# First layer norm of a decoder trunk: row statistics of two of three token chunks moved from VectorE's statistics instruction to ScalarE's accumulating passes

## The chip, the core and the metric

The kernel runs on one core of a Trainium2 chip. TensorE multiplies matrices out of SBUF into PSUM, VectorE and ScalarE do the elementwise work, GpSimd does a little of it, and the queue of SyncE starts nearly all transfers. The metric is the device time of one execution in microseconds. The time before is 1571.87 us, the median of three runs (1571.16 to 1574.35).

## The reference, cut to what matters

One decoder layer is computed for 1024 prompt tokens and 32 sample tokens, together 1056 tokens of 1024 features. A head mixer (mLSTM and sparse attention) gives `mixed`; the change touches only the layer norm behind it.

```
x = layer_norm(ALPHA * x + g1 * mixed, ln_g[0], ln_b[0])
u2 = x * (1 + sc2) + sh2
ff = jnp.square(jax.nn.relu(u2 @ w_up)) @ w_down
x = layer_norm(ALPHA * x + g2 * ff, ln_g[1], ln_b[1])

def layer_norm(x, g, b):
    mu = x.mean(-1, keepdims=True)
    var = jnp.square(x - mu).mean(-1, keepdims=True)
    return (x - mu) * lax.rsqrt(var + LN_EPS) * g + b
```

## The kernel before

Activations lie transposed, features on the partitions. The 1056 tokens are cut into three chunks, c = 0, 1 and 2, of 384, 384 and 288 tokens. For each chunk the following is done.

- `wout_steps(c)` multiplies by w_out: eight output tiles, m = 0 to 7. Each of the eight weight tiles comes by a transfer into the single buffer `wst`, is cast by ScalarE into `wo..h` (L50), and VectorE writes the rest of the split into `wo..l` (L51). TensorE makes `po` (L354), VectorE adds the residual into `y` (L1135).
- `ln1(c)` first takes the chunk in tiles of up to 128 tokens, three to a chunk. For each tile TensorE transposes the eight `y` into two PSUM halves `pn` of 128x512 (L1245). Of these halves there are four buffers, so two tiles can be under way. Then `norm_rows` takes the statistics: VectorE's statistics instruction on each half (L1246), their aggregation (L1251), the addition of the epsilon (L113), GpSimd's power of -1/2 (L114), and VectorE's -mean*r (L1253). Last, ScalarE writes the normalised tile `xna` from the two halves (L1267). There are three `xna` buffers, as many as a chunk has tiles, so the tiles of a chunk reuse the buffers of the chunk before.
- The second half of `ln1(c)` is a loop over the eight feature tiles f: TensorE transposes back from the three `xna` into `pb` (L1301, two buffers), ScalarE applies gain and bias into `x1` (L1303, two buffers, named `x` in the rows), a transfer stores `x1` to `d_x1` (L1304), VectorE makes `uraw` (L1307), and ScalarE and VectorE split it into the operands `B11`, `B21`, `B22`. Behind chunks 1 and 2 sums of blocks (`t_sum`, L1364) follow, which the up-projection's seven products need.

A second form, `norm_rows_act`, is in use in the second layer norm at the end of the kernel, where the tiles are named `xnf` and `lstf`. It takes the sum of a half as a by-product of a copying ScalarE pass (L1276), makes minus the mean on VectorE (L1280), takes the sum of squares as a by-product of a ScalarE Square pass with minus the mean as its bias (L1282), makes variance, root and -mean*r (L1284, L113, L114, L1286), and then writes the normalised tile as the first form does (L1288). Both of the extra passes write their elementwise result into the tile `xn` as well, where the final pass overwrites it:

```python
ACT.activation(xn[0:rows, 512 * hf:512 * hf + 512], pts[hf][0:rows], AF.Identity,
               accum_out=st[0:rows, hf:hf + 1])
...
ACT.activation(xn[0:rows, 512 * hf:512 * hf + 512], pts[hf][0:rows], AF.Square, bias=nm,
               accum_out=s[:, 3 + hf:4 + hf])
```

The order of the calls in the program is `ln1(0)`, the rest of `wout_steps(1)`, `ln1(1)`, `wout_steps(2)`, `ln1(2)`, and then `up_early` for two of the up-projection's column blocks (`pu0e`, `pu1e`), whose products with `B11` and `B21` can begin before chunk 2 is done. When the program is built, the framework's planner puts the instructions of each engine in an order from a timeline that it simulates, with the program's order as priority; on the chip each engine then runs its list in order and waits where an operand isn't there.

Of the kernel before, what the change touches and what calls it, by code (L numbers as in the profile page):

```python
# [47 lines left out]
def split(nc, hi, lo, src):  # L48

    nc.scalar.copy(hi, src)  # L50
    nc.vector.tensor_tensor(out=lo, in0=src, in1=hi.bitcast(F32), op=ALU.subtract)  # L51
# [7 lines left out]
def _body(tc, nc, top, io, dbg):  # L59
    PE, ACT, DVE, POOL, SP = nc.tensor, nc.scalar, nc.vector, nc.gpsimd, nc.sync  # L60

    def pool(name, stack, bufs=1, space=None, side=None):
        kw = {}
        if space is not None:
            kw["space"] = space
        if side is not None:
            kw["side"] = side
        if space is not DRAM:
            kw["reuse_waits"] = "tile"
        return stack.enter_context(tc.tile_pool(name=name, bufs=bufs, **kw))  # L70

    def mk(p, shape, dt, tag, bufs=None, name=None):
        kw = {} if bufs is None else {"bufs": bufs}
        return p.tile(list(shape), dt, tag=tag, name=name or tag, **kw)
# [16 lines left out]
    def v4(x, t=4):  # L91
        return x.rearrange("p (b t) -> p b t", t=t)

    def bc(x, n):

        return x.unsqueeze(2).broadcast_to([x.shape[0], x.shape[1], n])
# [131 lines left out]
    for i in range(16):  # L228
# [5 lines left out]
        if i % 2:  # L234
            o = kvx[:, :, 8 * i - 8:8 * i + 8].rearrange("p x (a n) -> p a x n", a=2)
# [590 lines left out]
    for h in range(2):  # L826
# [23 lines left out]
        for j in range(2):  # L850
            o, p = 512 * j, 288 * j
# [278 lines left out]
    ys = {}  # L1130
# [42 lines left out]
    while not (qs.end and qp.end and dn_end):  # L1173
# [4 lines left out]
        if best <= t and (behind or dn_at > t):  # L1178
            if rp <= t:
                qp.need = None  # L1180
                c = qp.pull()
            else:
                qs.need = None
                c = qs.pull()
# [54 lines left out]
    p4 = pool("p4", s4_, side="right")  # L1239
    ps4 = pool("ps4", s4_, space=PSUM)  # L1240

    def norm_half(pts, st, cols, hf, rows):

        for x in range(4):
            PE.transpose(pts[hf][0:rows, 128 * x:128 * x + 128], cols[4 * hf + x], ident)  # L1245
        DVE.bn_stats(st[0:rows, 6 * hf:6 * hf + 6], pts[hf][0:rows])  # L1246

    def norm_stats(st, rows):

        mv, rs = st[0:rows, 12:14], st[0:rows, 14:16]  # L1250
        DVE.bn_aggr(mv, st[0:rows, 0:12])  # L1251
        rstd_of(rs[:, 0:1], mv[:, 1:2], EPA)
        DVE.tensor_scalar(rs[:, 1:2], mv[:, 0:1], rs[:, 0:1], -1.0, op0=ALU.mult, op1=ALU.mult)  # L1253
        return mv[:, 0:1], rs[:, 0:1], rs[:, 1:2]

    def norm_tiles(pp, name):
        return (mk(pp, [128, 1024], F32, "xn", bufs=3, name=f"xn{name}"),
                mk(pp, [128, 16], F32, "lst", bufs=3, name=f"lst{name}"))

    def norm_rows(pp, pts, name, cols, rows):  # L1260

        xn, st = norm_tiles(pp, name)
        for hf in range(2):
            norm_half(pts, st, cols, hf, rows)
        _, r, nmr = norm_stats(st, rows)
        for hf in range(2):
            ACT.activation(xn[0:rows, 512 * hf:512 * hf + 512], pts[hf][0:rows], AF.Identity, scale=r, bias=nmr)  # L1267
        return xn
# [22 lines left out]
    def ln1(c):  # L1291
        t0, n = CH[c]
        tts = [(o, min(128, n - o)) for o in range(0, n, 128)]
        xns = []
        for o, rows in tts:
            pts = [mk(ps4, [128, 512], F32, "t", bufs=4, name=f"pn{c}{o}{hf}") for hf in range(2)]
            xns.append(norm_rows(p4, pts, f"a{c}{o}", [ys[c, m][:, o:o + rows] for m in range(8)], rows))
        for f in range(8):
            pt = mk(ps4, [128, 512], F32, "t2", bufs=2, name=f"pb{c}{f}")
            for (o, rows), xn in zip(tts, xns):  # L1300
                PE.transpose(pt[:, o:o + rows], xn[0:rows, 128 * f:128 * f + 128], ident[0:rows, 0:rows])  # L1301
            x1 = mk(p4, [128, 384], F32, "x1", bufs=2, name=f"x1{c}{f}")
            ACT.activation(x1[:, 0:n], pt[:, 0:n], AF.Identity, scale=lnT[:, 0, f:f + 1], bias=lnT[:, 1, f:f + 1])  # L1303
            SP.dma_start(d_x1[:, f, t0:t0 + n], x1[:, 0:n])  # L1304
            u = uraw[:, f, t0:t0 + n]
            np_ = min(n, 1024 - t0)
            DVE.tensor_scalar(u[:, 0:np_], x1[:, 0:np_], sc2p[:, f, 0:1], ada[:, 3, f, 0:1], op0=ALU.mult, op1=ALU.add)  # L1307
            if np_ < n:
                DVE.tensor_tensor(out=v4(u[:, np_:n]), in0=v4(x1[:, np_:n]), in1=bc(sc2p[:, f, 1:9], 4), op=ALU.mult)
                DVE.tensor_tensor(out=v4(u[:, np_:n]), in0=v4(u[:, np_:n]), in1=bc(ada[:, 3, f, 1:9], 4), op=ALU.add)  # L1310
            for a, b, name in ((t0, min(t0 + n, TH), "B21" if f >= 4 else "B11"), (max(t0, TH), t0 + n, "B22")):
                if a < b and (a < TH or f >= 4 and c < 2):
                    hi, lo = (x[:, f % 4, a % TH:a % TH + b - a] for x in ops[name])
                    split(nc, hi, lo, uraw[:, f, a:b])
            if f >= 4 and c:
                a, b = ((0, 240), (240, TH))[c - 1]
                t_sum("T3", f - 4, a, b, POOL if c == 1 else DVE)
                t_sum("T2", f - 4, a, b, POOL if c == 1 else DVE)
                if c == 2 and f < 4 + KT:
                    split(nc, ops["T2"][0][:, f - 4], ops["T2"][1][:, f - 4], ublock("T2", f - 4, 0, TH))  # L1320
# [37 lines left out]
    def ublock(name, k, a, b):  # L1358
        f, t = blk[name]
        return uraw[:, f + k, t + a:t + b]  # L1360

    def t_sum(name, k, a, b, eng):
        x, y, op = sum_of[name]
        eng.tensor_tensor(out=ublock(name, k, a, b), in0=ublock(x, k, a, b), in1=ublock(y, k, a, b), op=op)  # L1364

    TENG = POOL
    ln1(0)
    for _ in fill or wout_steps(1):
        pass
    ln1(1)  # L1370
    for _ in wout_steps(2, pq):
        pass
    operand(pq, "T2")
    ln1(2)
    spre = ExitStack()
    ppre = pool("pre", spre)
# [291 lines left out]
    def banks(name):  # L1668
        nt[0] += 1
        return [wtile(f"pnf{name}{hf}") if nt[0] % 2 else mk(psd, [128, 512], F32, "t", bufs=2, name=f"pnf{name}{hf}")  # L1670
                for hf in range(2)]
# [35 lines left out]
    pts = [banks(t) for t in last]  # L1707
    xns = [norm_tiles(pf, f"f{t}") for t in last]
# [149 lines left out]
```

## Time and profile before

| | |
|---|---|
| time, median of 3 runs | 1571.87 us |
| the profiled execution's time | 1571.22 us |
| its span | 1569.5 us |
| busy share: TensorE, VectorE, ScalarE, GpSimd | 95%, 67%, 42%, 19% |
| first layer norm, first transposition to last `x1` | 785.95 to 857 us |

The page gives shares over the whole span. The layer norm is one stretch of 71 us in it, which the windows and timelines below show by itself. The profiled execution took 1.7 us more than its span, and lies 0.65 us below the median.

### The profile page before, as it was taken

What the parts mean: (1) busy time and instruction counts of PE and PEld (TensorE: products, weight loads), DVE (VectorE), ACT (ScalarE), POOL (GpSimd) and SP (SyncE); (2) the same over time, 40 slices, a digit from 0 to 9 for tenths busy, and PEclk for the clock granted to TensorE, in tenths of its full rate; (3) what the DMA queues carried; (4) which work ended last, traced back from release to release, by engine and by line L of the source; (5) the groups of instructions that cost most, each with busy time, mean ns of one, the idle gap of its engine ahead of it and who ended that gap; (6) DMA issues with size and microseconds to landing.
All of it is one profiled execution on the core that took longest, in us unless ns stands there. A gap on an engine that the chain in (4) does not pass through costs nothing.

```text
span 1569.5 us, 30107 instructions
## 1 busy us (share of the span) xinstructions
PE 1492.4 (95%) x11647; PEld 1433.4 (91%) x11647; DVE 1054.1 (67%) x2340; ACT 657.6 (42%) x1332; POOL 300.6 (19%) x387
## 2 busy tenths in 40 slices
PE   6899999999999999899998799999999999998985
PEld 5788988999999998798897799999999999998985
DVE  2421132386676677977688887767668788979867
ACT  2422132375665566645466322222226433333363
POOL 0000000143224243443103300000001120304044
PEclk9989999999999999999999899999999999999997
DMA  8757477521020323323564566323323341422352
GB/s 294 276 188 266 115 195 243 149 73 48 26 78 19 98 67 120 89 61 102 170 215 137 188 217 221 110 99 108 103 83 129 136 150 56 131 88 54 111 107 85
DMA packets 112987, 204.11 MB, mean 130 GB/s; under 512 B 18530, under 2 KB 63499, under 8 KB 111915
## 3 DMA queue, kind: packets, MB, share of 16 engines
q1 hardware_dynamic: 109242, 196.67, 38.6%
q0 software_dynamic: 2304, 4.20, 1.8%
q8 instruction: 92, 1.51, 0.4%
q10 hardware_dynamic: 1296, 1.31, 0.2%
q14 instruction: 53, 0.43, 0.1%
HBM read 162.95 MB, written 46.07 MB: 133 GB/s over the span
## 4 chain that ended last, share of the span: by engine, by line
PE 75%; DVE 12%; DMA 6%; issue 3%; ACT 2%; POOL 1%; SPq 1%; ACTq 0%; DVEq 0%; POOLq 0%
PE p L1329 20%; PE pj L354 15%; PE pd L1564 11%; PE po L354 6%; PE o L1060 4%; PE pt L1019 4%; PE S L979 4%; DMA wada<-in_w_ada 3%; PE pA L298 2%; DVE oplT L51 2%; DVE ophT L51 2%; DVE A L1575 2%; PE ada L149 1%; DVE acc L1569 1%; PE hidS L277 1%
## 5 line engine op out<-in xcount | busy, mean ns | idle before, releaser
L1564 PE MATMUL pd<-oplT,ophT 128*128 128x264 f32 x2352 | 291.9, 287 | 8.5 <-ACT acc L1583 4.4
L1564 PEld LDWEIGHTS pd<-oplT,ophT 128*128 128x128 f32 x2352 | 290.9, 190 | 9.4 <-DVE ophT L51 4.8
L1002 POOL TENSOR_SCALAR P<-P,l,sg 128x64 f32<-128x64 f32 (+8 forms) x192 | 129.1, 686 | 173.7 <-DVE l L999 154.8
L51 DVE TENSOR_TENSOR PTl<-pt,PTh 128x512 fp32r<-128x512 f32 (+1 forms) x160 | 101.9, 643 | 31.2 <-ACT PTh L50 30.6
L996 ACT ACTIVATE P<-P,mn 128x640 f32<-128x640 f32 (+7 forms) x128 | 94.3, 737 | 67.7 <-DVE mn L823 64.3
L354 PE MATMUL pj<-uh,wt_l 128*128 128x384 f32 (+1 forms) x576 | 120.3, 333 | 0.0
L50 ACT CAST PTh<-pt 128x512 fp32r<-128x512 f32 (+1 forms) x160 | 86.7, 550 | 79.7 <-PE pt L1019 78.9
L354 PE MATMUL pj<-uh,wt_h 128*128 128x384 f32 (+1 forms) x576 | 115.9, 331 | 0.7 <-ACT rw L468 0.7
L354 PE MATMUL pj<-ul,wt_h 128*128 128x384 f32 (+1 forms) x576 | 116.5, 329 | 0.0
L1575 POOL TENSOR_TENSOR A<-A,A 128x1024 f32<-128x1024 f32 x7 | 24.1, 3455 | 476.7 <-DVE ophT L51 475.5
L50 ACT CAST ophT<-A 128x1024 fp32r<-128x1024 f32 x49 | 51.3, 1049 | 133.7 <-PE pd L1564 85.5
L354 PEld LDWEIGHTS pj<-uh,wt_l 128*128 128x128 f32 x576 | 95.7, 190 | 2.8 <-issue 2.4
L1019 PE MATMUL pt<-ident,P 128*128 128x128 f32 x592 | 95.6, 275 | 1.1 <-POOL P L1002 1.0
L354 PEld LDWEIGHTS pj<-uh,wt_h 128*128 128x128 f32 x576 | 93.6, 189 | 3.2 <-issue 1.6
L354 PEld LDWEIGHTS pj<-ul,wt_h 128*128 128x128 f32 x576 | 94.4, 188 | 2.0 <-issue 1.6
L1569 DVE TENSOR_TENSOR acc<-acc,pd 128x264 f32<-128x264 f32 (+1 forms) x126 | 61.9, 512 | 28.7 <-PE pd L1564 28.7
L1060 PE MATMUL o<-PTh,V 128*128 128x256 f32 x264 | 78.8, 305 | 0.5 <-DVE ob L1079 0.4
L1060 PE MATMUL o<-PTl,V 128*128 128x256 f32 x264 | 72.4, 295 | 3.2 <-DVE PTl L51 2.8
L1019 PEld LDWEIGHTS pt<-ident,P 128*128 128x128 f32 x592 | 70.0, 141 | 4.8 <-POOL P L1002 2.0
L51 DVE TENSOR_TENSOR oplT<-B,oplT 128x1056 fp32r<-128x1056 f32 x49 | 72.4, 1478 | 0.4 <-ACT oplT L50 0.2
L979 PE MATMUL S<-K,QH 128*128 128x512 f32 (+3 forms) x200 | 71.2, 360 | 1.1 <-DVE mn L823 0.7
L51 DVE TENSOR_TENSOR ophT<-A,ophT 128x1024 fp32r<-128x1024 f32 x49 | 66.0, 1349 | 7.6 <-ACT ophT L50 7.6
(1105 smaller groups left out, 3464.5 us busy)
## 6 DMA issues: line engine op xcount, KB each, us to landing
wada<-in_w_ada SPq DMA_DIRECT2D x48, 512.0 KB
aw<-in_w_up SPq DMA_DIRECT2D x32, 512.0 KB
d_r<-C SPq DMA_DIRECT2D x62, 264.0 KB
B<-d_r SPq DMA_DIRECT2D x28, 528.0 KB
A<-in_w_down SPq DMA_DIRECT2D x28, 512.0 KB
wst<-in_w_t SPq DMA_DIRECT2D x24, 512.0 KB
wst<-in_w_out SPq DMA_DIRECT2D x24, 512.0 KB
w<-in_cmp_w SPq DMA_DIRECT2D x4, 1024.0 KB
```

Of the source, the lines that this page charges most:

```text
L50: nc.scalar.copy(hi, src)
L51: nc.vector.tensor_tensor(out=lo, in0=src, in1=hi.bitcast(F32), op=ALU.subtract)
L354: PE.matmul(ps[:, 0:n], lhsT=a[:, k, :], rhs=b[:, k, t0:t0 + n], start=(i == 0 and k == 0), stop=(i == 2 and k == 7))
L979: PE.matmul(S[:, 0:w], lhsT=Q[:, r], rhs=K[j][:, k0 + c0:k0 + c0 + w], start=(i == 0), stop=(i == 1))
L996: ACT.activation(P[:, o:o + n], P[:, o:o + n], AF.Exp, bias=mn[:, br:br + 1], scale=-1.0, accum_out=l[:, br:br + 1])
L1002: POOL.tensor_scalar(P[:, a:b], P[:, a:b], l[:, x:x + 1], sg[:, qb, y:y + 1], op0=ALU.mult, op1=ALU.mult)
L1019: PE.transpose(pt[:, 256 * x + 128 * e:256 * x + 128 * e + 128], P[:, o:o + 128], ident)
L1060: PE.matmul(op, lhsT=vv, rhs=ps[e][:, 256 * x:256 * x + 256], start=(x0 + x == 0 and e == 0), stop=(x0 + x == len(bl) - 1 and e == 1))
L1329: PE.matmul(ps[:, 0:HH], lhsT=w[a][:, k], rhs=ops[name][b][:, k, HH * h:HH * h + HH], start=(i == 0 and k == 0), stop=(i == 2 and k == 3))
L1564: PE.matmul(ps[h][:, 0:HH], lhsT=x[:, 128 * m:128 * m + 128], rhs=y[:, HH * h:HH * h + HH], start=(i == 0), stop=(i == len(mms) - 1))
L1569: DVE.tensor_tensor(out=out, in0=out, in1=x, op=ALU.add)
L1575: eng.tensor_tensor(out=r[out], in0=r[a], in1=r[b], op=op)
```

## The change

For chunks 0 and 1, `ln1` calls `norm_rows_act` in the place of `norm_rows`. Chunk 2 keeps `norm_rows`. Nothing else is edited; the function called is already there.

```diff
@@ -1294,7 +1294,7 @@
         xns = []
         for o, rows in tts:
             pts = [mk(ps4, [128, 512], F32, "t", bufs=4, name=f"pn{c}{o}{hf}") for hf in range(2)]
-            xns.append(norm_rows(p4, pts, f"a{c}{o}", [ys[c, m][:, o:o + rows] for m in range(8)], rows))
+            xns.append((norm_rows if c == 2 else norm_rows_act)(p4, pts, f"a{c}{o}", [ys[c, m][:, o:o + rows] for m in range(8)], rows))
         for f in range(8):
             pt = mk(ps4, [128, 512], F32, "t2", bufs=2, name=f"pb{c}{f}")
             for (o, rows), xn in zip(tts, xns):
```

## Rows read from the trace of the kernel before

**Rows 1.** The page, busy time of the engines over the whole span.
```profile
PE 1492.4 (95%) x11647; PEld 1433.4 (91%) x11647; DVE 1054.1 (67%) x2340; ACT 657.6 (42%) x1332; POOL 300.6 (19%) x387
```
**Rows 2.** Windows, five of seven stretches: us, then busy us (and instructions) of each engine.
```profile
785.50:802.50 17.00, 17.00 (x116) 16.86 (x115) 13.11 (x26) 8.62 (x11) 1.67 (x3) 1.00 0.59 191
802.50:817.10 14.60, 14.60 (x118) 14.60 (x117) 13.15 (x34) 9.67 (x17) 1.27 (x2) 1.00 0.70 215
817.10:830.00 12.90, 12.90 (x102) 12.90 (x102) 11.45 (x27) 9.40 (x15) 0.55 (x1) 1.00 0.74 242
...
846.00:856.40 10.40, 10.34 (x71) 8.70 (x69) 7.90 (x29) 5.54 (x13) 0.82 (x2) 0.94 0.43 140
856.40:884.50 28.10, 15.62 (x97) 14.92 (x97) 25.96 (x42) 13.94 (x27) 21.15 (x8) 0.82 0.30 100
```
**Rows 3.** The chain that ended last, in order of time: start us, us, what.
```profile
834.79 0.68 ACT x L1303
835.49 1.90 DMA d_x<-x
...
840.09 0.09 ACT xna L1267
```
**Rows 4.** TensorE's timeline: start us, us, line, operation, out<-in, count [idle before].
```profile
785.95 1.91 PE L1245 MATMUL pn<-ident,y 128*128 128x128 f32 x16
...
816.60 0.49 PE L1301 MATMUL pb<-ident,xna 128*128 128x128 f32 x3
...
820.50 0.60 PE L1245 MATMUL pn<-ident,y 128*128 128x128 f32 x4
...
824.07 1.30 PE L354 MATMUL po<-m2T2h,wo26h 128*128 128x288 f32 x8
...
839.10 0.49 PE L1301 MATMUL pb<-ident,xna 128*128 128x128 f32 x3
```
**Rows 5.** ScalarE's timeline around the layer norm, same columns.
```profile
812.75 1.05 ACT L50 CAST wo24h<-wst 128x1024 fp32r<-128x1024 f32 x1 [3.44 <-DMA wst<-in_w_out]
...
818.05 2.78 ACT L1267 ACTIVATE xna<-pn,lsta 128x512 f32<-128x512 f32 x4
...
821.27 1.06 ACT L50 CAST wo26h<-wst 128x1024 fp32r<-128x1024 f32 x1
...
828.32 1.44 ACT L1267 ACTIVATE xna<-pn,lsta 128x512 f32<-128x512 f32 x2
...
839.41 2.79 ACT L1267 ACTIVATE xna<-pn,lsta 128x512 f32<-128x512 f32 x4
```
**Rows 6.** Tile lsta (statistics of the first layer norm): count, ns min/median/max, first and last start.
```profile
L1246 DVE BATCH_NORM_STATS2 lsta<-pn x18: 646/690/698, 787.2 to 841.9; 128x6 f32<-128x512 f32 x16, 32x6 f32<-32x512 f32 x2
...
L1251 DVE BATCH_NORM_AGGREGATE lsta<-lsta x9: 189/199/210, 789.6 to 842.6; 128x2 f32<-128x12 f32 x8, 32x2 f32<-32x12 f32 x1
...
L1253 DVE TENSOR_SCALAR lsta<-lsta x9: 201/205/214, 791.9 to 843.8; 128x1 f32<-128x1 f32 x8, 32x1 f32<-32x1 f32 x1
```
**Rows 7.** VectorE's timeline: the last step of one tile's statistics.
```profile
827.69 0.21 DVE L1253 TENSOR_SCALAR lsta<-lsta 128x1 f32<-128x1 f32 x1 [0.66 <-POOL lsta L114]
```
**Rows 8.** Tiles xnf and lstf (second layer norm, the form with sums), as Rows 6.
```profile
L1276 ACT ACTIVATE xnf<-pnf x14: 581/594/600, 1504.3 to 1548.2; 128x512 f32<-128x512 f32 x10, 112x512 f32<-112x512 f32 x2, 48x512 f32<-48x512 f32 x2
...
L1282 ACT ACTIVATE xnf<-pnf,lstf x14: 671/697/712, 1510.7 to 1551.8; 128x512 f32<-128x512 f32 x10, 112x512 f32<-112x512 f32 x2, 48x512 f32<-48x512 f32 x2
...
L1280 DVE TENSOR_SCALAR lstf<-lstf x7: 197/214/214, 1510.3 to 1550.8; 128x1 f32<-128x1 f32 x5, 112x1 f32<-112x1 f32 x1, 48x1 f32<-48x1 f32 x1
```
**Rows 9.** ScalarE's timeline in the second layer norm.
```profile
1510.13 0.59 ACT L1276 ACTIVATE xnf<-pnf 128x512 f32<-128x512 f32 x1
...
1510.70 0.69 ACT L1282 ACTIVATE xnf<-pnf,lstf 128x512 f32<-128x512 f32 x1
...
1511.37 0.70 ACT L1282 ACTIVATE xnf<-pnf,lstf 128x512 f32<-128x512 f32 x1
...
1514.86 1.45 ACT L1288 ACTIVATE xnf<-pnf,lstf 128x512 f32<-128x512 f32 x2 [1.36 <-DVE lstf L1286]
```

## The prediction

> **What bounds the kernel now.** I read the page first: over the whole span TensorE is busy for 95%, ScalarE for 42% [rows 1]. Such averages would make a ScalarE addition look free, so I cut the layer norm's stretch into windows by what happens in it [rows 2]. From 785.5 to 830 us TensorE has work all the time. VectorE is busy for 13.11 of 17.0 us, 13.15 of 14.6 and 11.45 of 12.9, so it is nearly full; ScalarE has 8.62 of 17.0, 9.67 of 14.6 and 9.40 of 12.9, so it has 8.4 us free in the first window, 4.9 in the second and only 3.5 in the third. In the last window, 856.4 to 884.5, TensorE works for 15.6 of 28.1 us: it waits there for the operands that come out of the layer norm. A delay of the norm is thus not absorbed behind it.
>
> Next the chain that ended last. Ahead of the rows shown it is TensorE's work without a break; from 834.79 it lies on the norm: an `x` pass of ScalarE, 1.90 us for a store of `x1` to free its buffer, a wait for ScalarE's `xna` [rows 3]. The reader is to see that from there the norm sets the end, and TensorE follows.
>
> Then I asked what starts each chunk. The three `xna` buffers tie the chunks together. The last transposition back of chunk 0 runs from 816.60 to 817.09, and chunk 1's first `xna` pass starts at 818.05; the last of chunk 1 starts at 839.10, and chunk 2's `xna` starts at 839.41 [rows 4, 5]. So the norm is a relay: chunk 0's loop over f frees the buffers at 817.1, chunk 1 is normalised until 829.8 (828.32 + 1.44), its loop runs until 839.4, and only then chunk 2 is written. What makes one leg longer makes the end later by about as much.
>
> **The change part by part.** Removed, for six tiles of 128 tokens: 12 statistics instructions of 0.690 us, 6 aggregations of 0.199 and 6 multiplications of 0.205 [rows 6], together 8.28 + 1.19 + 1.23 = 10.7 us of VectorE. Added there: three small ones a tile at the 0.214 us of the second norm's [rows 8], 18 x 0.214 = 3.9 us. VectorE is relieved of 6.8 us. The epsilon and GpSimd's power stay.
>
> Added to ScalarE: four passes a tile. One takes 0.594 us for the sum and 0.697 us for the squares [rows 8], but they overlap: in a row they start 0.57 us apart (1510.13 to 1510.70) and 0.67 apart (1510.70 to 1511.37) [rows 9]. A tile costs 2 x 0.57 + 2 x 0.67 = 2.48 us, a chunk 7.4 us, the change 14.9 us. Nothing is added to a DMA queue, but SyncE's queue orders weight loads behind casts, so a late cast makes the next load late.
>
> There is a second part that no duration shows: the statistics now write into `xna`. In the kernel before, the statistics of chunk 1's first two tiles are taken by VectorE long before the buffers are free, from PSUM into `lsta`, and at 818.05 four ready passes follow each other for 2.78 us [rows 5]. After the change the first sum can't start before 817.1. So chunk 1's 7.4 us of ScalarE work all fall into the leg from 817.1 to 829.8, instead of being spread.
>
> Chunk 0's leg. The first transpositions start at 785.95 [rows 4], `xna` has no earlier user, and 8.4 us of idle ScalarE stand against 7.4 us of new work. From both sides: were only the chain of passes to count, it would take two tiles' sums and squares (4.96 us), the first tile's two final passes (half of 2.78, 1.39), the third tile's transpositions (0.9, from 1.91 for two tiles), its sums and squares (2.48), a gap for its statistics (1.36, as at 1514.86 [rows 9]) and its final passes (1.44): 12.5 us, and 0.9 for the first transpositions, 13.4 instead of 17.0, a gain of up to 3.6. If the casts of w_out tiles and of the mixer's output that lie in this window go ahead of the passes, a loss of about 3 (three casts of 1.05 [rows 5]). I take 0, as the two nearly cancel and the new work just fits.
>
> Chunk 1's leg, the term that decides. Here 7.4 us meet 3.5 us of free ScalarE [rows 2], because the leg also holds the last passes of chunk 0's loop and casts of weights. The excess is 3.9 us. Below, the bare chain of 12.5 us ends no earlier than the 12.7 us that the leg takes now, since the third tile's statistics wait for VectorE today (transpositions at 820.50, last step at 827.69 [rows 4, 7]) and would no longer: 0. Above, nothing overlaps: 7.4. I take 3.9, by the window.
>
> Chunk 0's loop between them takes 14.6 us, where chunk 2's takes 10.4 [rows 2]. It has a wait of 3.44 us of ScalarE for a weight's transfer in it [rows 5], and VectorE loses the statistics of two chunk 1 tiles there (4 x 0.69). Bounds: 0 and -4.2. I take 0: that wait is for a transfer, which this change doesn't hasten. Behind 830 the relay is the same work, so 0; its order can shift by a pass or two, 1 us either way.
>
> The sum: 0 + 3.9 + 0 + 0 on the profiled execution's 1571.22 us is 1575.1. That execution lies 0.65 us below the median of the runs, so I give 1575.8 us, 0.25% slower.
>
> Here a rule speaks for the change. VectorE's 13.15 of 14.6 us are the row [rows 2]. The Trainium skill (Perfetto Trace Analysis, Optimizing Scalar/DVE Operations) says that work may move from a saturated VectorE to ScalarE. By that rule the relief of VectorE is what counts; by the row of the leg after, ScalarE's room is what counts. Rows support the first half of it, and I make the case that it decides a rival below.
>
> **The rivals.**
>
> *VectorE was the brake, and the norm gets faster.* For it: the third tile of chunk 1 takes 7.4 us (820.50 to 827.90) from transposition to its last statistic [rows 4, 7] with a small share of it work. Against it: the buffers free at 817.1 set the start. It decides if chunk 0's leg and loop together gain more than chunk 1's leg loses. With half of the leg's bound (-1.8), half of the loop's (-2.1) and chunk 1 at its lower bound (0): 1571.87 - 3.9 = 1568.0 us. The Trainium skill's rule above is this case.
>
> *Covered.* ScalarE's other work in the third window, such as the casts for `up_early`, which no one needs at once, gets out of the way, and chunk 1's leg loses some 1 us: 1572.9 us, no change that can be measured. For it: the bare chain fits. Against: the cast of `wo26h` at 821.27 is needed by TensorE at 824.07 [rows 4, 5], so not every cast can go.
>
> *TensorE runs dry.* If a pair of tiles' sums and squares (4.96 us) goes ahead of that cast, which ends at 822.33 and has 1.7 us of room, TensorE waits 3.3 us; chunk 2's `y` get late by it. One such wait hides behind the later relay; two of them (6.6) exceed the 3.9 that the relay is late by 2.7, and give 1578.5 us.
>
> **How the numbers follow.** The forecast (3.1 to 8 us slower) has 0.42; running dry 0.10; covered, within 0.2%, 0.32; faster 0.16. A measurement of this kernel can tell about 0.2%, 3.1 us, from no change. The forecast's size lies close to that bound, so a part of its spread is counted as no change: the covered case runs from -2 to +3. Slower 0.52, same 0.32, faster 0.16. The likeliest case's own range is 1574.5 to 1580. The range over all cases reaches from 1568 (the faster rival) to 1581.5 (chunk 1 at 7.4, chunk 0 at half of its loss, 1.5, and half a us of order: 1571.87 + 9.4 is 1581.3).
>
> **What the profile of the changed kernel would show.** Right: no statistics instruction of VectorE for chunks 0 and 1 (6 instead of 18 for `lsta`); 12 sum and 12 square passes, some 0.6 and 0.7 us each, chunk 1's first not before chunk 0's last transposition back; chunk 1's last `xna` pass some 4 us later than 829.8, the loops behind as long as now, and the whole later part shifted by that. ScalarE nearly full between the first sum of chunk 1 and its last `xna`. Wrong: chunk 0's last transposition back well before 816, which would be VectorE's relief; TensorE idle before 832, the rival that runs dry; or an order of the planner that differs so much in this stretch that legs can't be matched, which the trace of before can't show and which is the main risk.

## The result, and the profile after

Ten runs of each kernel on one chip: 1579.99 us after the change (1574.95 to 1588.64) and 1570.30 us before (1563.76 to 1576.86). The ratio is 1.0072, with a 95% interval of 1.0053 to 1.0091: the change costs 11.3 us by the ratio (8.3 to 14.3). The medians lie 9.7 us apart, which is within that interval. The forecast had the sign, but the loss is nearly three times the 3.9 us that it gave. That 1579.99 us lies within the stated range of 1568 to 1581.5 is in part luck: the kernel before came out at 1570.30 us here and not at the 1571.87 that the forecast started from, and 11.3 us on top of that would have been 1583.2.

The profiled execution after took 1584.49 us, its span 1582.7 us. First its page's busy line, which answers to [rows 1]:

```profile
PE 1496.9 (95%) x11647; PEld 1438.6 (91%) x11647; DVE 1051.2 (66%) x2334; ACT 673.7 (43%) x1380; POOL 299.5 (19%) x387
```

The shares hardly move: VectorE gives 2.9 us and ScalarE takes 16.1. (The durations of VectorE's instructions on `lsta` do add up to 6.8 us less, 10.5 against 17.3, as was foreseen; busy time counts once what overlaps.) Nothing here tells of 11 us. The instructions of the tiles `lsta` and `xna` are the ones foreseen, 6 statistics instructions where [rows 6] have 18, and twelve passes of each kind at nearly the durations of [rows 8]:

```profile
L1282 ACT ACTIVATE xna<-pn,lsta x12: 677/718/738, 790.3 to 836.4; 128x512 f32<-128x512 f32 x12
...
L1280 DVE TENSOR_SCALAR lsta<-lsta x6: 204/212/215, 789.3 to 835.4; 128x1 f32<-128x1 f32 x6
...
L1246 DVE BATCH_NORM_STATS2 lsta<-pn x6: 668/689/699, 836.7 to 852.1; 128x6 f32<-128x512 f32 x4, 32x6 f32<-32x512 f32 x2
```

```profile
L1276 ACT ACTIVATE xna<-pn x12: 582/602/618, 788.0 to 834.7; 128x512 f32<-128x512 f32 x12
```

The windows by the stages of [rows 2]: chunk 0's norm, chunk 0's loop, chunk 1's norm, chunk 1's loop, chunk 2's norm and loop, and the wait for the sums behind it. The last three figures of a row are TensorE's granted clock as a share of full speed, the DMA share and GB/s.

```profile
787.40:806.80 19.40, 19.40 (x136) 19.37 (x135) 11.66 (x26) 17.05 (x36) 1.67 (x3) 1.00 0.63 201
806.80:821.50 14.70, 14.70 (x118) 14.70 (x118) 11.17 (x27) 10.14 (x16) 0.00 (x0) 1.00 0.72 227
821.50:840.80 19.30, 15.15 (x119) 14.48 (x117) 13.55 (x39) 17.08 (x40) 2.41 (x4) 1.00 0.41 134
840.80:849.00 8.20, 7.24 (x39) 6.46 (x37) 6.26 (x17) 5.90 (x16) 2.31 (x4) 0.58 0.40 144
849.00:867.60 18.60, 16.08 (x92) 12.92 (x91) 13.12 (x40) 11.28 (x23) 4.78 (x7) 0.82 0.29 98
867.60:894.80 27.20, 14.39 (x98) 14.15 (x97) 25.32 (x40) 14.80 (x29) 20.83 (x8) 0.78 0.35 119
```

In the norms of chunks 0 and 1 ScalarE is now the busier of the two: 17 of 19 us, VectorE 11.7 and 13.6. Chunk 0's norm takes 19.4 us where it took 16.6 (its window in [rows 2] begins 0.45 us ahead of it), chunk 1's 19.3 where it took 12.7. In the latter TensorE, which had no gap there, is idle for 4.15 us, and the granted clock is 1.00, so no clock is involved in this leg. Behind the idle time it is 0.58, mostly the lower of the two levels (1.2 GHz); more on that below. The loop of chunk 0 between them takes what it took, 14.7 us.

To compare kernels I read the same milestones from the timelines of TensorE and ScalarE of every profile, counted from chunk 0's first transposition. "Norm" is the end of a chunk's last final pass into `xna`, "loop" the end of its last transposition back, "T" the start of the first product that uses the sums, where the stretch of the layer norm hands over to the up-projection.

```
us from the first transposition    norm0  loop0  norm1  loop1  norm2  loop2     T
before                              16.6   31.1   43.8   53.6   59.9   70.4   98.5
after                               19.4   34.2   53.4   61.6   69.2   80.3  107.4
e1  chunk 0 only                    21.3   36.9   51.0   58.1   68.1   80.6  108.2
e2  chunk 1 only                    15.4   30.6   52.1   59.5   68.3   77.2  104.2
e3  after, six buffers              20.8   40.9   38.9   55.5   60.2   70.0   98.6
e4  before, six buffers             15.9   32.5   38.0   51.8   68.4   75.9  104.0
e5  sums beside the tile            20.1   36.7   50.4   57.7   68.4   77.9  106.1
e6  passes added, unused            22.4   37.3   54.1   61.4   72.1   82.9  111.6
e7  less work for VectorE           13.1   27.8   40.8   52.1   65.0   72.9  101.1
e8  neutral edit                    15.8   31.1   43.8   53.6   59.9   70.5   98.6
e9  e4, sums on VectorE             16.6   32.5   37.8   50.7   66.9   74.5  102.7
e10 e2, six buffers                 15.8   36.6   44.8   53.9   60.2   70.6   98.7
e11 before, sums on VectorE         15.4   31.1   44.4   53.6   60.7   69.2   97.3
e12 e10, sums on VectorE            16.1   36.6   44.5   54.0   60.7   70.4   98.5
```

The change loses 2.8 us up to norm0, 0.2 in loop0, 6.6 from loop0 to norm1 (19.3 against 12.7), gets 1.6 back in loop1, loses 1.3 and 0.6 in chunk 2's norm and loop, and gets 1.0 back behind it: 8.9 us at T. That lies within the interval of the measured loss. The spans of these two executions differ by more, 13.2 us: 1.4 of it lies ahead of the norm's start and 2.9 behind T, where nothing was edited.

The granted clock over chunk 1's loop, chunk 2's norm and chunk 2's loop is 0.58, 0.92 and 0.75 after the change and 1.00, 0.83 and 0.94 before. In e8, which runs every engine's instructions in the order of before, it is 1.00 in all three, and those three legs take the same to 0.1 us; so that much of a clock doesn't move these milestones. In chunk 2's loop after the change TensorE is busy for 10.7 of 11.1 us at 0.75, and in e1, the longest, for 12.2 of 12.5 at 0.62. There the low clock may have cost some of the 0.6 and 2.0 us by which that loop is longer; no run shows it apart.

ScalarE's timeline shows what the passes stand between (the small reads of the accumulators are among the lines left out):

```profile
793.90 1.29 ACT L50 CAST m2T2h<-mr 128x576 fp32r<-128x576 f32 x2
795.03 1.10 ACT L50 CAST wo20h<-wst 128x1024 fp32r<-128x1024 f32 x1
795.99 2.84 ACT L1288 ACTIVATE xna<-pn,lsta 128x512 f32<-128x512 f32 x4
...
805.29 1.45 ACT L1288 ACTIVATE xna<-pn,lsta 128x512 f32<-128x512 f32 x2
...
822.26 0.58 ACT L1276 ACTIVATE xna<-pn 128x512 f32<-128x512 f32 x1
...
823.40 0.68 ACT L1303 ACTIVATE x<-pb,lnT 128x384 f32<-128x384 f32 x1
...
825.10 1.07 ACT L50 CAST wo27h<-wst 128x1024 fp32r<-128x1024 f32 x1
826.03 0.55 ACT L50 CAST B21h<-uraw 128x384 fp32r<-128x384 f32 x1
826.45 0.72 ACT L1282 ACTIVATE xna<-pn,lsta 128x512 f32<-128x512 f32 x1
...
827.78 0.55 ACT L50 CAST B21h<-uraw 128x384 fp32r<-128x384 f32 x1
...
828.86 0.73 ACT L1282 ACTIVATE xna<-pn,lsta 128x512 f32<-128x512 f32 x1
...
829.52 1.09 ACT L50 CAST wu0h<-wst 128x1024 fp32r<-128x1024 f32 x1
830.46 1.51 ACT L1288 ACTIVATE xna<-pn,lsta 128x512 f32<-128x512 f32 x2
...
839.35 1.45 ACT L1288 ACTIVATE xna<-pn,lsta 128x512 f32<-128x512 f32 x2 [2.21 <-DVE lsta L1286]
```

And TensorE's, same columns:

```profile
798.30 1.55 PE L354 MATMUL po<-m1mh,wo17l 128*128 128x384 f32 x8
799.69 0.60 PE L1275 MATMUL pn<-ident,y 128*128 128x128 f32 x4
...
821.02 0.49 PE L1301 MATMUL pb<-ident,xna 128*128 128x128 f32 x3
...
831.35 0.66 PE L1275 MATMUL pn<-ident,y 128*128 128x128 f32 x4 [0.85 <-ACT xna L1288]
...
840.18 0.44 PE L1301 MATMUL pb<-ident,xna 128*128 128x128 f32 x2 [3.30 <-ACT xna L1288]
...
894.75 1.25 PE L1329 MATMUL p<-T2h,ah0s 128*128 128x264 f32 x4 [6.49 <-ACT ah0s L50]
```

The buffers of `xna` are free at 821.51 (821.02 + 0.49). Before the change the final passes of two tiles start 0.96 us later [rows 4, 5]. Now eight statistics passes go ahead of them, and between those stand casts and an `x` pass that were put there in ScalarE's order: the first final pass starts 8.20 us behind the first sum (822.26 to 830.46). The third tile's transpositions need a `pn` pair that the first tile's final pass gives back, so they start 9.84 us after the buffers are free (831.35); in the kernel before it was 3.4 (817.09 to 820.50). That is 6.4 of the leg's 6.6 us. Then the third tile's own chain follows, 9.5 us where it was 9.3 (820.50 to 829.76), and TensorE waits 3.30 us at its end.

In chunk 0's leg no buffer of `xna` is missing. Tile 0's last statistic starts at 793.88 and takes 0.21 us, but two casts of `m2T2h` and one of `wo20h` stand ahead of its final passes, which start at 795.99. Counted from the first transposition that is 8.63 us, though, and in the kernel before it was 8.40. The leg's 2.8 us come from the third tile. The same events before:

```profile
794.35 1.45 ACT L1267 ACTIVATE xna<-pn,lsta 128x512 f32<-128x512 f32 x2
...
801.06 1.45 ACT L1267 ACTIVATE xna<-pn,lsta 128x512 f32<-128x512 f32 x2 [1.78 <-DVE lsta L1253]
```

```profile
796.37 1.03 PE L1245 MATMUL pn<-ident,y 128*128 128x128 f32 x8
```

The third tile's transpositions start 12.33 us after the first one where they started at 10.42, 1.9 us later. TensorE isn't idle; in its new order they stand behind the products with `wo17l`, though tile 0's two final passes have given the `pn` pair back at 797.49. From there to the end of the tile's final passes it takes 7.05 us (799.69 to 806.74) in the place of 6.14 (796.37 to 802.51), 0.9 us more for the longer chain.

### The profile page after: what moved, and what is told of

It reads as the page before. It is cut to its first block, busy times and chain, and to the rows that moved or that the text cites. A ratio compares the mean times of both kernels' runs of the same rounds, so it can differ in the third digit from the quotient of the medians.

```text
span 1582.7 us, 30153 instructions
## 1 busy us (share of the span) xinstructions
PE 1496.9 (95%) x11647; PEld 1438.6 (91%) x11647; DVE 1051.2 (66%) x2334; ACT 673.7 (43%) x1380; POOL 299.5 (19%) x387
## 4 chain that ended last, share of the span: by engine, by line
PE 74%; DVE 13%; DMA 6%; ACT 3%; issue 2%; SPq 1%; POOL 1%; DVEq 0%; ACTq 0%; POOLq 0%
PE p L1329 19%; PE pj L354 15%; PE pd L1564 11%; PE po L354 5%; PE o L1060 4%; PE pt L1019 4%; PE S L979 4%; DMA wada<-in_w_ada 3%; DVE oplT L51 2%; DVE ophT L51 2%; DVE A L1575 2%; PE pA L298 1%; DMA w<-in_cmp_w 1%; PE ada L149 1%; DVE acc L1569 1%
```

## The experiments

Times are medians; a ratio is to runs of the kernel before on the same chip.

**The two halves, e1 and e2.**

```diff
- xns.append(norm_rows(p4, pts, f"a{c}{o}", ...
+ xns.append((norm_rows_act if c == 0 else norm_rows)(p4, pts, f"a{c}{o}", ...     # e1
+ xns.append((norm_rows_act if c == 1 else norm_rows)(p4, pts, f"a{c}{o}", ...     # e2
```

> The sums on ScalarE for chunk 0 alone. Theory (each chunk's leg of the relay grows by the ScalarE work that finds no room in it; 2.8 us for chunk 0 and 6.6 us for chunk 1 as the changed kernel's trace shows them): 1 to 4 us slower than the kernel before. Rival (the extra ScalarE work costs the same wherever it lies, half of the change's 10 to 11 us): 5 us slower. Rival (the planner's new order costs, whatever is edited): 8 to 11 us slower.

> The sums on ScalarE for chunk 1 alone. Theory (legs): 6 to 9 us slower than the kernel before, well above chunk 0 alone. Rival (the work costs the same wherever it lies): 5 us slower. Rival (new order of the planner): 8 to 11 us slower, like chunk 0 alone.

Chunk 0 alone: 1579.05 us against 1571.00, ratio 1.0046 (1.0024 to 1.0067), +9.7 us at T. Chunk 1 alone: 1577.65 us, 1.0032 (1.0012 to 1.0053), +5.7 at T. Chunk 1 cost nearly what was expected, 5.0 us by the ratio (1.9 to 8.3), and norm1 comes 8.3 us later. But it was to cost far more than chunk 0, and it didn't: chunk 0 cost 7.2 us (3.8 to 10.5) in the place of 1 to 4, its norm ends 4.7 us later, and norm2 8.2 us later. Both halves lose, and the losses don't add up (15.4 at T against 8.9 for both), so they share a cause or hide behind each other. Both intervals hold the 5 us of the rival by which the work costs the same wherever it lies; e3 settles that one.

**More buffers, e3 and e4.** Each tile of `xna` and `lsta` gets a buffer that no chunk before it holds, with the change (e3) and without it (e4).

```diff
- return (mk(pp, [128, 1024], F32, "xn", bufs=3, name=f"xn{name}"),
-         mk(pp, [128, 16], F32, "lst", bufs=3, name=f"lst{name}"))
+ return (mk(pp, [128, 1024], F32, "xn", bufs=6 if name[0] == "a" else 3, name=f"xn{name}"),
+         mk(pp, [128, 16], F32, "lst", bufs=6, name=f"lst{name}"))
```

> The changed kernel with six buffers for the normalised tiles and for the statistics of the first layer norm in the place of three, so that chunk 1's sums need not wait for chunk 0's last transposition back. Theory (the statistics write into the tile and so start late): most of chunk 1's 6.6 us comes back, 2 to 5 us slower than the kernel before. Rival (it is ScalarE's total work in the stretch): it stays 9 to 11 us slower.

> The kernel before, VectorE's statistics, with the same six buffers. If the three buffers make the relay that sets the end: 3 to 6 us faster than the kernel before, as chunk 1's loop can follow chunk 0's at once. Rival (the buffers are no bound, the products of w_out that feed chunk 2 are): no change, within 2 us.

e3: 1572.67 us, 1.0006 (0.9986 to 1.0026), +0.1 at T. More came back than expected: the whole loss is gone, with all 24 passes still on ScalarE. ScalarE's timeline of e3 (first transposition at 783.45):

```profile
812.47 0.72 ACT L1282 ACTIVATE xna<-pn,lsta 128x512 f32<-128x512 f32 x1
...
818.39 1.53 ACT L1288 ACTIVATE xna<-pn,lsta 128x512 f32<-128x512 f32 x2
...
836.12 1.45 ACT L1267 ACTIVATE xna<-pn,lsta 128x512 f32<-128x512 f32 x2
```

Chunk 1's squares are taken at 812, while chunk 0's loop still reads its own tiles (loop0 ends at 824.4, 783.45 + 40.9), and its norm is done at 38.9 instead of 53.4. So ScalarE had room for the passes in the stretch as a whole; what it lacked was a free buffer to write into.

e4: 1575.56 us, 1.0019 (0.9995 to 1.0044), +5.5 at T: no gain (the 3 to 6 us expected lie outside the interval), although norm1 comes 5.9 us earlier. The relay of buffers isn't what alone sets the end in the kernel before. Norm2 comes 8.5 us *later*; more on that at e7 and e9. With six buffers in both, the kernel with the change is thus 5.5 us ahead at T; how much of that is the order that the planner drew for each, these two runs don't tell.

**Load without the chain, e6; chain without the buffer, e5.** In e6 VectorE's statistics stay and are used; the four accumulating passes per tile run besides and write into the tile, their sums unused. In e5 the changed kernel's accumulating passes write into spare half tiles, and `xna` is touched by the final passes alone.

```diff
+ if name[:2] in ("a0", "a1"):                                                     # e6
+     acc = mk(pp, [128, 4], F32, "acc_", bufs=3, name=f"acc_{name}")
+     for x in range(4):
+         hf = x % 2
+         ACT.activation(xn[0:rows, 512 * hf:512 * hf + 512], pts[hf][0:rows],
+                        AF.Square if x > 1 else AF.Identity, accum_out=acc[0:rows, x:x + 1])

+ def dump(hf):                                                                    # e5
+     if name[0] == "a":
+         return mk(pp, [128, 512], F32, "dump", bufs=2, name=f"dump{name}{hf}")[0:rows]
+     return xn[0:rows, 512 * hf:512 * hf + 512]
- ACT.activation(xn[0:rows, 512 * hf:512 * hf + 512], pts[hf][0:rows], AF.Identity,
-                accum_out=st[0:rows, hf:hf + 1])
+ ACT.activation(dump(hf), pts[hf][0:rows], AF.Identity, accum_out=st[0:rows, hf:hf + 1])
  ...                                                                              # the Square pass likewise
```

> The kernel before, with VectorE's statistics in use, and the four accumulating ScalarE passes for each tile of chunks 0 and 1 added, writing into the normalised tile, their sums used by nobody: the load and the late start without the chain of sum, mean, squares, root. Theory (the late passes themselves fill chunk 1's leg): 6 to 10 us above the kernel before, nearly as the changed kernel. Rival (the hops between ScalarE, VectorE and GpSimd in the chain are the cost): 0 to 4 us above.

> The changed kernel with one edit: the elementwise results of the sum and square passes of the first layer norm go into two spare half tiles instead of the normalised tile, which keeps its three buffers. Theory (chunk 1's leg grows because the passes write into the tile and so wait for chunk 0's last transposition back): chunk 1's statistics are taken ahead, its leg is within 2 us of the kernel before's 12.7, and the time is 2 to 5 us above the kernel before (chunk 0's leg stays longer). Rival (ScalarE's total work in the stretch, or the longer chain of hops itself): 9 to 11 us above, as the changed kernel.

e6: 1583.15 us against 1570.10, 1.0078 (1.0050 to 1.0107), +13.1 at T, more than the 6 to 10 expected. The final passes wait for no sum, and the loss is all there; chunk 1's leg is 16.8 us. In ScalarE's timeline chunk 1's first extra pass starts 1.2 us after the buffers are free (822.84, 785.52 + 37.3), and the first final pass 6.48 us behind it:

```profile
824.04 0.58 ACT L1269 ACTIVATE xna<-pn 128x512 f32<-128x512 f32 x1
...
829.94 0.66 ACT L1269 ACTIVATE xna<-pn 128x512 f32<-128x512 f32 x1
830.52 0.84 ACT L1273 ACTIVATE xna<-pn,lsta 128x512 f32<-128x512 f32 x1
```

So the longer chain of hops (sum, mean, squares, root) is not needed for chunk 1's late start; passes that must wait for the buffers suffice. Chunk 0's leg, where none waits for a buffer, lost 5.8 us here.

e5: 1577.82 us, 1.0050 (1.0028 to 1.0072), +7.6 at T. Here my expectation mostly fell. Its own point came true: four final passes start 1.35 us after loop0 ends (816.73), and chunk 1's leg is 13.7 us instead of 19.3, near the 12.7 of before.

```profile
818.08 2.77 ACT L1292 ACTIVATE xna<-pn,lsta 128x512 f32<-128x512 f32 x4
...
829.03 1.44 ACT L1292 ACTIVATE xna<-pn,lsta 128x512 f32<-128x512 f32 x2 [1.85 <-DVE lsta L1290]
...
837.82 2.80 ACT L1267 ACTIVATE xna<-pn,lsta 128x512 f32<-128x512 f32 x4
```

But chunk 0's leg is 20.1 us (16.6 before), its loop 16.5 (14.6), and chunk 2's leg 10.7 (6.3). The loss moved to other legs. So taking the wait out of chunk 1's leg is not enough to get the time back. The two spare halves are a resource too, and the engines' orders were drawn anew; which of the two made chunk 2 late this run doesn't tell apart.

**Was VectorE the brake? e7, with e8 as its yardstick.** e7 takes some 5 us of statistics from VectorE in chunks 0 and 1 (12 instructions of about 0.29 us in the place of 0.69) by leaving out three quarters of each half's columns, and gives ScalarE nothing. e8 changes the count of `lsta` buffers alone.

```diff
- DVE.bn_stats(st[0:rows, 6 * hf:6 * hf + 6], pts[hf][0:rows])                     # e7
+ DVE.bn_stats(st[0:rows, 6 * hf:6 * hf + 6], pts[hf][0:rows, 0:n_stat[0]])        # n_stat[0]: 128 for c < 2, else 512
- mk(pp, [128, 16], F32, "lst", bufs=3, name=f"lst{name}"))                        # e8
+ mk(pp, [128, 16], F32, "lst", bufs=6, name=f"lst{name}"))
```

> The kernel before with VectorE's statistics of chunks 0 and 1 taken over the first 128 of each half's 512 columns: some 5 us of VectorE's work are left out and nothing is added, so the statistics are of a quarter of the features. Theory (VectorE was no brake, the buffers' relay is): within 2 us of the kernel before. Rival (VectorE was the brake of this stretch): 3 to 5 us faster.

> The kernel before with six instead of three buffers for the small statistics tiles alone, which adds and removes no instruction: how far the planner's order by itself moves the time. Theory (the legs explain the change): within 2 us of the kernel before. Rival (any edit draws a new order, and the new order is the cost): 4 us or more off, in either direction.

e8: 1570.04 us, 1.0006 (0.9986 to 1.0027), and T and five of the other six milestones are within 0.1 us of before; norm0 comes 0.8 us earlier. Every engine's order is that of before. So a difference of a microsecond at T is likely one of the kernel and not of the run, as far as one repetition tells; at norm0 it need not be.

e7: 1572.99 us, 1.0018 (0.9998 to 1.0038), +2.6 at T. VectorE's relief is real: norm0 comes 3.5 us earlier and norm1 3.1. It is given back in chunk 2, whose leg grows from 6.3 to 12.9 us. Part of it is seen in GpSimd's queue, which begins with sums; the powers that chunk 2's statistics need stand behind and between them:

```profile
832.40 0.70 POOL L1367 TENSOR_TENSOR uraw<-uraw 128x240 f32<-128x240 f32 x1 [13.05 <-PE pb L1304]
833.39 1.41 POOL L1367 TENSOR_TENSOR uraw<-uraw 128x240 f32<-128x240 f32 x2 [0.30 <-DVE uraw L1310]
834.76 0.71 POOL L114 TENSOR_TENSOR lsta<-lsta,nhalf 128x1 f32<-128x1 f32 x1
```

In the kernel before, the powers run first:

```profile
837.47 1.38 POOL L114 TENSOR_TENSOR lsta<-lsta,nhalf 128x1 f32<-128x1 f32 x2 [9.81 <-DVE lsta L113]
838.84 3.08 POOL L1364 TENSOR_TENSOR uraw<-uraw 128x240 f32<-128x240 f32 x4
```

**Is it GpSimd's queue? e9 to e12.** The sums of chunk 1 go to VectorE, on e4 (e9), on before (e11) and on e10 (e12). e10 is chunk 1's half of the change with six buffers.

```diff
- t_sum("T3", f - 4, a, b, POOL if c == 1 else DVE)       # e9, e11, e12; T2 likewise
+ t_sum("T3", f - 4, a, b, DVE)
```

> The kernel before with six buffers, as in the fourth experiment, and chunk 1's eight block sums moved from GpSimd to VectorE. In the fourth experiment six of these sums stood in GpSimd's queue ahead of the powers of chunk 2's first tiles, and the stretch from the first transposition to the first product with T took 104.0 us against 98.5. Theory (GpSimd's queue gives the gain of the earlier chunks back in chunk 2's leg): the stretch is 95 to 99 us, the time from 3 us faster to 1 us slower than the kernel before. Rival (chunk 2's leg is long there for another reason, such as a late cast): it stays at 102 to 105 us, 3 to 5 us slower.

> The sums on ScalarE for chunk 1 alone and six buffers. Theory (writing into a tile that is still in use is the cost of chunk 1's share, VectorE keeps chunk 0's leg short): the stretch is 97 to 101 us, the time within 3 us of the kernel before. Rival (ScalarE's work costs by itself): 104 us as without the buffers, 4 to 6 us slower.

> The kernel before, three buffers, with chunk 1's eight block sums moved from GpSimd to VectorE: the control for the ninth experiment. Theory: the powers of chunk 2 stood ahead of these sums already, so nothing is gained, and VectorE gets 3 us more work behind chunk 1: 0 to 3 us slower. Rival (GpSimd's sums hold up VectorE or the powers in the kernel before too): 2 us faster or more.

> The tenth experiment's kernel with chunk 1's block sums on VectorE too. Theory: no power of chunk 2 can stand behind a sum, the stretch is 95 to 99 us and the time from 3 us faster than the kernel before to no change. Rival (VectorE, which gets the sums, sets chunk 2's leg): 2 us or more slower than the tenth experiment.

| | us (before 1569.09) | ratio, 95% interval | T against before |
|---|---|---|---|
| e9 | 1571.61 | 1.0016 (0.9994 to 1.0038) | +4.2 |
| e10 | 1567.24 | 0.9999 (0.9980 to 1.0017) | +0.2 |
| e11 | 1567.69 | 0.9989 (0.9967 to 1.0011) | -1.2 |
| e12 | 1567.87 | 0.9996 (0.9978 to 1.0014) | 0.0 |

e10 repeats e3 with half of the change: chunk 1's 5.7 us are gone when its tiles have buffers of their own. e11's T comes 1.2 us earlier where 0 to 3 us slower was expected; its time can't be told from no change. e9 is a miss. No sum of chunk 1 is in GpSimd's way, and norm2 is still 7.0 us late. Its VectorE timeline shows another queue: the second to fourth statistics of chunk 2 stand behind the split of an up-projection weight, which waits for ScalarE.

```profile
828.77 0.69 DVE L1246 BATCH_NORM_STATS2 lsta<-pn 128x6 f32<-128x512 f32 x1
...
831.22 1.23 DVE L51 TENSOR_TENSOR wu1l<-wst,wu1h 128x1024 fp32r<-128x1024 f32 x1 [1.76 <-ACT wu1h L50]
...
832.68 0.69 DVE L1246 BATCH_NORM_STATS2 lsta<-pn 128x6 f32<-128x512 f32 x1
...
834.06 1.28 DVE L1246 BATCH_NORM_STATS2 lsta<-pn 128x6 f32<-128x512 f32 x2
...
836.65 0.20 DVE L1251 BATCH_NORM_AGGREGATE lsta<-lsta 128x2 f32<-128x12 f32 x1
...
837.84 0.40 DVE L1364 TENSOR_TENSOR uraw<-uraw 128x240 f32<-128x240 f32 x1
...
838.87 0.20 DVE L113 TENSOR_SCALAR lsta<-lsta 128x1 f32<-128x1 f32 x2
```

```profile
839.18 2.87 POOL L114 TENSOR_TENSOR lsta<-lsta,nhalf 128x1 f32<-128x1 f32 x2 [21.77 <-DVE lsta L113]
```

ScalarE's cast in turn waits 2.12 us for the weight's transfer. Counted from the first transposition, the fourth statistic ends 52.9 us in, 3.3 later than in the kernel before. From there to the end of the two powers it takes 6.7 us (835.34 to 842.05) where it took 3.3, as sums that were moved now stand between the statistics on VectorE and the powers themselves take 2.87 us in the place of 1.38. So the move also cost part of what it was to bring. Chunk 2 is thus tied to the weights that come in beside it, by whatever place they have in the queues. In the six kernels whose T lies between 97.3 and 98.7 (before, e3, e8, e10, e11, e12), norm2 comes at 59.9 to 60.7, whenever norm1 came (38.9 to 44.8). I read this as a second bound just behind the relay. e11 and e12 show that taking the sums from GpSimd does nothing by itself. No version here beats the kernel before by what a measurement can tell.

## Why the prediction was off, point by point

**The mechanism held for chunk 1's leg.** The statistics passes write into `xna`, so chunk 1's first sum can't start before chunk 0's last transposition back: it started at 822.26, the buffers were free at 821.51. The legs behind follow, and the end is later. With buffers of their own the same passes cost nothing that can be measured (e3, e10); the leg is near its old length when the passes write elsewhere (e5, 13.7 us), and long when nobody uses their sums (e6, 16.8). So the cause of this leg's 6.6 us is shown. That the wait for the buffers is the cause of the whole loss is not: e5 takes it away and still loses 7.6 us at T. The durations were right too (0.602 and 0.718 us where 0.594 and 0.697 were taken).

**The step that failed first: "Chunk 1's leg, the term that decides", taken as 3.9 us.** It measured 6.6 us, in e2 8.8 (52.1 - 30.6 against 12.7). I set 7.4 us of passes against 3.5 us of free ScalarE as if the free time could be moved to where the passes needed it. It couldn't: of the 8.20 us between the first sum and the first final pass about 4.9 are passes and 3.3 are casts and an `x` pass that stand between them in ScalarE's order, and the third tile can't start until the first tile's final pass has given `pn` back. My upper bound, 7.4, "nothing overlaps", was the better guide, and e2 lies above even that.

**The second step: "Chunk 0's leg", taken as 0.** It measured +2.8 us, +4.7 in e1 (against e8, which has the order of before, it is 3.6; norm0 and loop0 together are 3.0 against either). The prediction let a loss of about 3, from casts ahead of the passes, cancel against a chain that could have been faster. Neither is what happened. The casts moved tile 0's final passes by 0.2 us only; TensorE's new order put the third tile's transpositions 1.9 us later, and that tile's chain got 0.9 us longer and not shorter. That the loss is near the 3 us named is luck. The planner's order, which the prediction called its main risk, is the larger part of this leg. That the leg's ScalarE total fits (17.05 of 19.4 us) says nothing about the order.

**The third: "Behind 830 the relay is the same work, so 0", 1 us either way.** Chunk 2's own leg and loop lost 1.9 us here, more in e1 and e5, and the loop of chunk 1 gave 1.6 back. Some of the 1.9 may be the lower granted clock in that loop (0.75 against 0.94), which the prediction didn't consider. The legs together, 2.8 + 0.2 + 6.6 - 1.6 + 1.9 - 1.0 (between loop2 and T), make 8.9, where the forecast had 3.9.

**Two readings.** VectorE was not "nearly full" in the first window: 13.11 of 17.0 us is 77%. And those 17.0 us begin 0.45 us ahead of the first transposition, so the faster chain could have gained 3.2 us at most and not 3.6.

**Loop 0 as 0** was right (+0.2). VectorE's load there fell from 13.15 to 11.17 us and the loop took no less time.

**The rivals.** "VectorE was the brake" fell: e7 relieved VectorE without any other cost, got the early norms that this rival foresaw, and no faster kernel. The Trainium skill (Perfetto Trace Analysis, Optimizing Scalar/DVE Operations) says that moving work from a saturated VectorE to ScalarE may make sense; the rows here don't bear it out: 13.15 of 14.6 us busy was no bound. "Covered" fell with the time. "TensorE runs dry" foresaw idle before 832 by a late weight cast; TensorE has 0.85 us there, and the 3.30 us at 840.18 are a wait for `xna`, so the relay and not that rival.

**What stays open.** Why chunk 0's half alone costs as much as the whole, and why chunk 2 is late in e1, e4 and e5, I read only from the order of the queues, and that is argued and not shown. The planner drew that order anew with each edit but e8's, and no run could hold it fixed while one wait was changed. That e3's result comes from the buffers and not from a lucky order rests on e10 and e12 doing the same; against it stands e4, where six buffers without the change are 5.5 us late.

## What to carry to other kernels

Ask where a moved pass writes its result, even one that is thrown away: if it is the buffer of a relay, the pass can't start before the relay's turn, and the receiving engine's free time ahead of that is worth nothing. Free time within a leg can't be moved to where it is needed either: count what stands between the new passes in the engine's order, and what the first of them gives back late. And measure an edit of less than one per cent between two events of the trace, with a neutral edit beside it, as well as by the whole time.

## What was not expected of the hardware

The whole time scatters more than the stretch under study. The kernel before gave 1565.39 to 1582.61 us in 35 runs on the chip of e1 to e4, but with the same order of instructions T came at 98.5 and 98.6 us in two executions whose times were 1571.22 and 1574.74 us. The scatter arises elsewhere: the first transposition starts at 780.05 us in e5's profile and at 787.36 in that of the changed kernel, and up to there every engine runs the same instructions in the same order in both.

VectorE's smallest operations can wait for GpSimd's large ones. In e7 four of GpSimd's sums run from 854.90 for 5.44 us, 1.36 us each. VectorE's timeline has the same addition, which reads two operands, before and during them, 0.18 and 1.30 us:

```profile
852.87 0.18 DVE L1312 TENSOR_TENSOR uraw<-x,sc2p 128x32 f32<-128x32 f32 x1
...
857.83 1.30 DVE L1312 TENSOR_TENSOR uraw<-x,sc2p 128x32 f32<-128x32 f32 x1
```

The Trainium skill (SBUF — State Buffer, Who interferes with whom) says that the two engines share a pair of ports that one of them holds for a whole instruction. The rows agree: the small addition takes about as long as one of GpSimd's sums.
